# Where the gates' double steps fall among the units of dilated attention

## The chip, the core and the metric

One core of one Trainium2 chip runs the whole kernel. The metric is the device time of one execution in microseconds, the median of several runs. The core's engines are TensorE (PE for matmuls, PEld for its weight loads), VectorE (DVE), ScalarE (ACT), GpSimd (POOL) and SyncE (SP), which here only issues DMAs; ACT issues some too.

## What is computed

One hybrid decoder layer over 1024 positions of width 1024. One input projection feeds two attention groups of 8 heads each, latent attention (MLA) and a dilated sliding-window attention. Each group's output is multiplied by a SiLU gate, which is its own 512 columns of the projection. Both are concatenated, projected and added to the input under a LayerNorm.

```
h = x @ w_in
c_q, c_kv, k_rope, g_a, q_b, k_b, v_b, g_b = split(h)
y_a = mla_attention(c_q, c_kv, k_rope, ...) * silu(g_a)
y_b = dilated_attention(q_b, k_b, v_b) * silu(g_b)
mix = concatenate([y_a, y_b])
x   = layernorm(ALPHA * x + mix @ w_out)
```

## The kernel before

**Precision.** Float32 products are made from a high and a low part each, in three passes (high by high, high by low, low by high), so a product of one 128 x 512 tile over 1024 input rows takes 24 matmuls.

**Stages in time.** Projections of q, k, the latents and v fill the time up to about 224 us. Then comes the dilated stage, to about 410 us, in which the gates are made as well. MLA attention follows, and the output projection with the LayerNorm ends the kernel.

**The dilated stage.** The loop at the end of the dilated part goes over 32 units, `steps`, each a head pair `hp`, a half of the sequence `s` and a block `u` of 128 queries. For a unit, `dil_scores` makes 20 small matmuls into two PSUM banks (`Sd`, L607 and L611), and DVE adds the mask and takes the maximum (`td`, L615). `dil_expo` makes the exponentials on ACT (L621). One unit later `dil_inv`, `dil_high` and `dil_low` turn them into a high and a low part in float16 on ACT, POOL and DVE (tile `p`), and after each second unit SP issues one transposing DMA for both (`ptd<-p`, L659). Five units later, after each fourth, `dil_values` multiplies the transposed probabilities by the values (`Od`, L687), and DVE multiplies by the gate (L688). The PSUM pool holds the scores of two units.

**The gates.** A gate `gate(m, s)` is 24 matmuls of `gP` (L523) with the weights `wg` of column block m and the half s of x, then a tanh on ACT (L533) and a product on DVE (L534). It is a generator that yields after its first 12 matmuls and at its end, so a gate has two steps. `GATES` has 16 of them, in the order (4,0), (4,1), (5,0), (5,1), (6,0), (6,1), (7,0), (7,1), (0,0), (0,1), (1,0), (2,0), (3,0), (3,1), (2,1), (1,1): 32 steps, counted here from 0. From (1,0) on each gate needs other weights than the one before it, except (3,1). Weights of a block come in two loads of 256 KB, each issued on ACT's queue, rounded on ACT (`wg`, L76) and subtracted on POOL (L77). The first of the next block is asked for after the first step of a gate, the second at its end (`GLOAD`). Three tiles hold halves of weights, two hold raw loads; wg2 and wg1 are loaded a second time for (2,1) and (1,1).

**The fillers.** `fillers()` strings the gates together. When gate (3,0) has ended, the first halves of x are no longer needed, and at the next step `latents_load` has SP load the latents `c`, `u` and the tables into their place. After the last gate `latents_first` makes MLA's first keys and queries in four more steps. The loop over units calls `next(fill)` once or twice per unit:

```
            for _ in range(1 + (n % 3 == 0 and n < 24)):
                next(fill, None)
```

In the same loop SP is given the transposes `qq` and `kk` for the next head pair (four, in units 9 to 12 and 17 to 20) and the loads `vA` and `vB` (in units 12, 20 and 28, counted from 0; those of the first pair come ahead of the loop).

**What sets the order.** The program's order is a priority. A planner lays out each engine's instructions ahead of time by simulated readiness, so an instruction can pass others that it thinks not ready; on the chip each engine then runs its own list strictly in that order. DMAs are given completion semaphores in turn, and the issue of one can wait for an earlier one's landing.

Of the kernel before, what the change touches and what calls it, by code (L numbers as in the profile page):

```python
# [40 lines left out]
def tile_hybrid_layer(ctx, tc, xT, xres, w_c, w_c2, w_vr, w_k, w_q, w_g, w_u, w_o,  # L41
# [285 lines left out]
    def pow2_find(vmx, nm, bank_=bank):  # L327
        m1 = small.tile([P, 1], F32, name=nm + "m1", tag="vm")
        nc.vector.tensor_reduce(m1, vmx, AX.X, ALU.max)
        find_pow2(m1, 2.0 ** -40, nm, bank_)  # L330

    def pow2(j, nm, inv, bank_=bank):

        e = common_pow2(nm, bank_)
        r = small.tile([P, 1], F32, name=nm + "r", tag="vm4")
        nc.vector.reciprocal(r, e)
        nc.vector.tensor_scalar(scl[:, j, 0:1], r, 2.0 ** 14, None, ALU.mult)
        nc.vector.tensor_scalar(scl[:, j, 1:2], e, 2.0 ** -14 * inv, None, ALU.mult)
# [63 lines left out]
    def mla_scales():  # L402

        ee, d = fs[:, 4:5], fs[:, 5:6]
        nc.vector.tensor_mul(ee, es[:, 1:2], es[:, 3:4])
        nc.vector.tensor_scalar(scl[:, 0, 1:2], ee, 2.0 ** -5 / PSC, None, ALU.mult)
        nc.vector.tensor_scalar(fs[:, 6:7], scl[:, 4, 1:2], 2.0, None, ALU.mult)
        nc.vector.scalar_tensor_tensor(d, ee, 2.0 ** 10, fs[:, 6:7], ALU.mult, ALU.max)
        nc.vector.reciprocal(fs[:, 6:7], d)
        nc.vector.tensor_scalar(fs[:, 2:3], fs[:, 6:7], 2.0 ** 15, None, ALU.mult)  # L410
        nc.vector.tensor_scalar(fs[:, 3:4], fs[:, 2:3], ee, 2.0 ** -24, ALU.mult, ALU.mult)
        nc.vector.tensor_mul(fs[:, 6:7], es[:, 0:1], es[:, 2:3])
        nc.vector.tensor_scalar(fs[:, 7:8], fs[:, 6:7], d, -SC_MLA * 2.0 ** -19, ALU.mult, ALU.mult)

    def load_qk(hp):
        QQ[hp] = qqp.tile([P, 2, T], F16, name=f"qq{hp}", tag="qq")
        KK[hp] = b8.tile([P, 3, T], F16, name=f"kk{hp}", tag="kk")
        for s in range(2):
            sync.dma_start_transpose(QQ[hp][:, :, half(s)], q_d[half(s), hp * 2 * P:(hp + 1) * 2 * P])
            yield  # L420
            sync.dma_start_transpose(KK[hp][:, :, half(s)], k_d[half(s), hp * 3 * P:(hp + 1) * 3 * P])
            yield
# [132 lines left out]
    def load_v(hp):  # L555
        VA[hp] = four(f"vA{hp}", [P, NB, 2, P])
        sync.dma_start(VA[hp], v_d[1][:, :, hp].rearrange("n p l c -> p n l c"))
        VB[hp] = four(f"vB{hp}", [P, 2, 4, 2, P])
        for c in range(4):
            sync.dma_start(VB[hp][32 * c:32 * c + 32].rearrange("a j r l c -> a (j r) (l c)"),  # L560
                           v_d[1][2 * c:2 * c + 2].rearrange("j (r a) g l c -> a g (j r) (l c)", a=32)[:, hp])
# [30 lines left out]
    def dil_scores(u_):  # L592

        hp, s, u = u_
        i, ns = 4 * s + u, 3 + s
        stt = ST[u_] = small.tile([P, 2, 4], F32, name=f"st{hp}{i}", tag="st", bufs=4)
        TD[u_] = four(f"td{hp}{i}", [P, 2, 512], F32)
        S = [ps_s.tile([P, 512], F32, name=f"Sd{hp}{i}{e}", tag="S")[:, :ns * P] for e in range(2)]

        for cls in range(2):  # L600
            for w, e in JOBS:
                rows = ME[e] if w else slice(0, P)
                q, kk = QQ[hp][rows, e], KK[hp][rows, 2 if w else e]
                if not cls:
                    rhs = kk[:, (i - 1) * P:(i + 1) * P] if i else \
                        kk[:, 0:P].unsqueeze(1).broadcast_to([rows.stop - rows.start, 2, P])
                    nc.tensor.matmul(S[e][:, (ns - 2) * P:], q[:, i * P:i * P + P], rhs, start=(w == 0), stop=False)  # L607
                    continue
                for r in range(4):
                    rhs = kk.rearrange("p (i r a) -> p r i a", r=4, a=32)[:, r, 0:4 * s + 4]  # L610
                    nc.tensor.matmul(S[e][32 * r:32 * r + 32, :(ns - 2) * P],  # L611
                                     q[:, i * P + 32 * r:i * P + 32 * r + 32], rhs, start=False, stop=(w == 1))
        mk = mdil[:, u if i else 4, (4 - ns) * P:]
        for e in range(2):
            nc.vector.tensor_tensor_reduce(TD[u_][:, e, :ns * P], S[e], mk, dsc[:, 1:2], BIG,  # L615
                                           ALU.add, ALU.min, stt[:, e, 0:1])
# [7 lines left out]
    def dil_inv(u_):  # L624
        stt = ST[u_]
        nc.vector.tensor_scalar(stt[:, :, 2], stt[:, :, 1], 1.0 / PSC, None, ALU.mult)
        nc.vector.reciprocal(stt[:, :, 3], stt[:, :, 2])  # L627

    def dil_high(u_):
        hp, s, u = u_  # L630
        ns = 3 + s
        if u % 2 == 0:
            P16[hp, s] = hp_.tile([P, 2, 2, 2, ns * P], F16, name=f"p16{hp}{s}{u}", tag="p16")
        p16 = P16[hp, s][:, u % 2]
        for e in range(2):
            t, h, sc = TD[u_][:, e, :ns * P], p16[:, e, 0], ST[u_][:, e, 3:4]
            w = WHO[u][e]
            if w == "P":
                nc.gpsimd.tensor_scalar(t, t, sc, 1.0, ALU.mult, ALU.mult)  # L639
                sc = 1.0  # L640
            if w == "Q":
                nc.gpsimd.tensor_scalar(h, t, sc, 1.0, ALU.mult, ALU.mult)
            else:
                nc.scalar.activation(h, t, AF.Copy, scale=sc)  # L644

    def dil_low(u_):
        hp, s, u = u_
        ns, p16 = 3 + s, P16[hp, s][:, u % 2]
        if u == 0:
            PTD[hp, s] = tp.tile([P, 4, 4 * ns, P], F16, name=f"ptd{hp}{s}", tag=f"pT{s}")  # L650
        for e in range(2):
            t = TD[u_][:, e, :ns * P]
            if WHO[u][e] == "P":
                nc.gpsimd.tensor_sub(p16[:, e, 1], t, p16[:, e, 0])  # L654
            else:
                nc.vector.scalar_tensor_tensor(p16[:, e, 1], t, ST[u_][:, e, 3:4], p16[:, e, 0],
                                               ALU.mult, ALU.subtract)
        if u % 2:
            sync.dma_start_transpose(PTD[hp, s][:, u - 1:u + 1].rearrange("p u z c -> p (u z) c"),  # L659
                                     P16[hp, s].rearrange("p u e l w -> p (u e l w)"))  # L660
# [52 lines left out]
    def gen_kpe(s, part):  # L713

        if part == 0:
            KR[s] = four(f"krd{s}", [P, 4, 4, 32], F32)
            for z in range(4):
                gcopy(KR[s][:, :, z], kru.rearrange("p n t d -> p n (t d)")[:, s * 4:s * 4 + 4])
            return
        p = gbank(f"kpt{s}")  # L720
        for j in range(4):
            nc.tensor.transpose(p[:, j * P:(j + 1) * P], KR[s][:, j].rearrange("p z d -> p (z d)"), ident)
        k, sc = four(f"kpe{s}", [P, 2, 512]), fs[:, 2:3]
        nc.scalar.activation(k[:, 0], p, AF.Copy, scale=sc)
        nc.vector.scalar_tensor_tensor(k[:, 1], p, sc, k[:, 0], ALU.mult, ALU.subtract)
        sync.dma_start(kp_d[:, :, half(s)], k)
# [149 lines left out]
    for n in range(ND + 5):  # L876
        cur = steps[n] if n < ND else None
        old = steps[n - 1] if 1 <= n <= ND else None
        if n == 2:
            pow2_find(krm, "kr", gbank)  # L880
        if n == 5:
            pow2(4, "kr", 2.0 ** 14, gbank)
            mla_scales()
            nc.vector.tensor_scalar(scl[:, 0, 2:3], scl[:, 0, 1:2], 0.5, None, ALU.mult)
        if 8 <= n < 12:
            gen_kpe((n - 8) // 2, n % 2)
        if cur:
            if cur[1:] == (0, 1) and 0 < cur[0] < PAIRS - 1:
                qks = load_qk(cur[0] + 1)
            next(qks, None)  # L890
            if cur[1:] == (1, 0) and cur[0]:
                load_v(cur[0])
            dil_scores(cur)
        if old:
            dil_inv(old)
            dil_high(old)
            dil_low(old)
        if cur:
            for e in range(2):
                dil_expo(cur, e)  # L900
            for _ in range(1 + (n % 3 == 0 and n < 24)):
                next(fill, None)
        if n == ND + 3:
            for _ in fill:
                pass
        m = n - DV
        if 0 <= m < ND and m % 4 == 3:
            dil_values(*steps[m][:2])
# [165 lines left out]
    for i in ROWS:  # L1074
# [5 lines left out]
        for c in range(2):  # L1080
            if i in HALVED:
                n = 1 + (i == ROWS[-1])
# [121 lines left out]
```

## Time and profile before

| | |
|---|---|
| median of 3 runs | 649.92 us (649.61 to 652.25) |
| the profiled execution | 647.9 us |
| its span | 646.1 us, 11108 instructions |
| mean granted clock of TensorE | 0.977 |
| PE, DVE, ACT, POOL busy | 91%, 60%, 49%, 45% |
| dilated stage | about 224 to 410 us |

The shares are means over all stages; the stretch table and the timelines of the section on rows show the dilated stage by itself. A timeline's row is a group of like instructions that follow each other on an engine: start and length in us, engine, line, operation, names as out<-in, shape, count, and in brackets the idle time before it and what ended it. An engine with a q is its queue, which issues DMAs; the length of an issue includes the time in which it could not go on.

### The profile page before, as it was taken

How to read it: one execution, taken by the hardware profiler on the slowest of the kernel's cores; microseconds unless marked ns; L12 is line 12 of the kernel's file. 1: busy time of each engine (PE TensorE's matmuls, PEld its weight loads, DVE VectorE, ACT ScalarE, POOL GpSimd, SP SyncE). 2: the span in 40 equal slices, each digit the busy share in tenths (PEclk: the TensorE clock that was granted, in tenths of full speed). 3: DMA queues.
4: the chain of work that ended last, by engine and by line, in shares of the span. 5: the costliest groups of instructions: out<-in, count | busy, mean ns of one | idle time of the engine just before them, and what ended most of it. 6: DMA issues, size and time to landing. Idle time of an engine off the chain costs nothing.

```text
span 646.1 us, 11108 instructions
## 1 busy us (share of the span) xinstructions
PE 590.4 (91%) x4046; PEld 432.2 (67%) x4046; DVE 388.8 (60%) x888; ACT 318.2 (49%) x643; POOL 293.0 (45%) x324
## 2 busy tenths in 40 slices
PE   8999998999999899999996997877988868899995
PEld 5888886788999466776764544443545436678884
DVE  4415318480541686645645576589888995365696
ACT  4452136554221486555635565487978695240000
POOL 3284754265431227734643555283739556440000
PEclk9999999999999999999997998899989998999998
DMA  6666037796012779995999999559887899752042
GB/s 198 196 200 196 23 97 204 219 284 181 33 66 72 264 235 140 181 223 98 220 287 232 198 187 234 115 112 203 159 153 147 172 199 230 160 152 81 18 162 98
DMA packets 199527, 107.10 MB, mean 166 GB/s; under 512 B 157616, under 2 KB 176176, under 8 KB 199344
## 3 DMA queue, kind: packets, MB, share of 16 engines
q1 hardware_dynamic: 195872, 100.68, 66.4%
q10 hardware_dynamic: 3600, 5.71, 3.4%
q8 instruction: 31, 0.51, 0.3%
q14 instruction: 24, 0.20, 0.1%
HBM read 48.70 MB, written 18.87 MB: 105 GB/s over the span
## 4 chain that ended last, share of the span: by engine, by line
PE 60%; DMA 15%; DVE 12%; ACT 4%; issue 4%; POOL 3%; SPq 1%; DVEq 0%; POOLq 0%; ACTq 0%
PE gP L523 11%; PE op L958 7%; PE cP L254 7%; PE acc L169 7%; PE qkP L130 7%; DMA pT<-ph 5%; PE vbA L130 4%; PE vbB L130 4%; PE op L1087 3%; DVE ph L847 3%; DVE p L815 2%; PE Od L687 2%; PE qg L770 2%; DMA ptd<-p 2%; PE Sd L607 2%
## 5 line engine op out<-in xcount | busy, mean ns | idle before, releaser
L523 PE MATMUL gP<-x,wg 128*128 128x512 f32 x384 | 99.0, 406 | 5.7 <-ACT wg L76 5.2
L523 PEld LDWEIGHTS gP<-x,wg 128*128 128x128 f32 x384 | 70.7, 191 | 22.8 <-ACT wg L76 5.6
L958 PE MATMUL op<-wo,ys 128*128 128x512 f32 x288 | 70.3, 399 | 1.8 <-POOL wo L77 1.4
L958 PEld LDWEIGHTS op<-wo,ys 128*128 128x128 f32 x288 | 54.2, 191 | 15.5 <-POOL wo L77 2.4
L820 ACT ACTIVATE p<-p,sm 128x128 f32<-128x128 f32 (+3 forms) x64 | 49.1, 768 | 24.5 <-DVE sm L815 20.3
L809 PE MATMUL S<-k,q 128*128 128x512 f16 (+3 forms) x288 | 53.4, 328 | 7.4 <-DVE sm L815 7.4
L254 PE MATMUL cP<-x,wc 128*128 128x512 f32 x240 | 56.7, 395 | 0.0
L815 DVE CUSTOM_DVE_ANT_0 p<-S,mask,fs 128x128 f32<-128x128 f32 (+3 forms) x64 | 51.0, 807 | 7.8 <-POOL ph L845 5.7
L254 PEld LDWEIGHTS cP<-x,wc 128*128 128x128 f32 x240 | 44.7, 188 | 10.3
L621 ACT ACTIVATE td<-td,st 128x384 f32<-128x384 f32 (+1 forms) x64 | 42.2, 660 | 15.2 <-DVE st L615 15.0
L809 PEld LDWEIGHTS <-q 128*128 128x128 f16 x288 | 25.6, 98 | 33.3 <-issue 9.6
L639 POOL TENSOR_SCALAR td<-td,st 128x384 f32<-128x384 f32 (+1 forms) x32 | 21.9, 690 | 55.2 <-DVE st L627 43.1
L615 DVE CUSTOM_DVE_ANT_0 td<-Sd,mdil,dsc 128x384 f32<-128x384 f32 (+1 forms) x64 | 41.3, 678 | 9.0 <-PE Sd L611 8.7
L169 PE MATMUL acc<-wq,x 128*128 128x512 f32 x192 | 45.1, 395 | 0.8 <-DVE x L156 0.8
L845 POOL TENSOR_TENSOR ph<-p,ph 128x256 f16<-128x256 f32 (+3 forms) x32 | 37.2, 1173 | 18.1 <-ACT ph L838 16.5
L130 PE MATMUL qkP<-wk,x 128*128 128x512 f32 x192 | 44.5, 393 | 0.0
L859 PE MATMUL O<-pT,v 128*64 128x256 f16 (+1 forms) x480 | 31.0, 271 | 14.6 <-DMA pT<-ph 14.6
L169 PEld LDWEIGHTS acc<-wq,x 128*128 128x128 f32 x192 | 36.0, 188 | 10.5 <-DVE x L156 1.3
L130 PEld LDWEIGHTS qkP<-wk,x 128*128 128x128 f32 x192 | 36.0, 188 | 8.2
L847 DVE SCALAR_TENSOR_TENSOR ph<-p,sm,ph 128x128 f16<-128x128 f32 (+3 forms) x32 | 36.7, 1157 | 7.7 <-ACT ph L838 7.7
L859 PEld LDWEIGHTS <-v 128*64 128x64 f16 x480 | 26.8, 113 | 20.5 <-issue 15.0
L654 POOL TENSOR_TENSOR p<-td,p 128x384 f16<-128x384 f32 (+1 forms) x32 | 35.4, 1118 | 8.3 <-ACT p L644 8.0
(313 smaller groups left out, 1140.9 us busy)
## 6 DMA issues: line engine op xcount, KB each, us to landing
u<-in_w_u_dram SPq DMA_DIRECT2D x20, 256.0 KB, 3.2
v_d<-v SPq DMA_DIRECT2D x16, 256.0 KB, 2.1
wor<-in_w_o_dram SPq DMA_DIRECT2D x8, 512.0 KB, 4.2
xr<-in_xres_dram SPq DMA_DIRECT2D x16, 256.0 KB, 3.1
out_dram<-xr SPq DMA_DIRECT2D x16, 256.0 KB, 2.1
xr<-in_xT_dram SPq DMA_DIRECT2D x15, 256.0 KB, 3.2
k_d<-k SPq DMA_DIRECT2D x8, 384.0 KB, 4.4
c_d<-c SPq DMA_DIRECT2D x10, 256.0 KB, 2.4
```

Source lines behind the costliest of these rows:

```text
L130: nc.tensor.matmul(d, xs[k][i // 4][:, a, (i % 4) * P:(i % 4) * P + P], w8[k][:, b, o:o + w], **flags(k, KD, (a, b)))
L169: nc.tensor.matmul(acc[i], xs[k][i // 4][:, a, (i % 4) * P:(i % 4) * P + P], ws[:, b, :512], start=(k == 0 and (a, b) == (0, 0)), stop=(k ...
L254: nc.tensor.matmul(dst, ww(k, a, m), xs[k][s][:, b], **flags(k, KD, (a, b)))
L523: nc.tensor.matmul(p, wg[k // 4][:, a, (k % 4) * P:(k % 4) * P + P], xs[k][s][:, b], **flags(k, KD, (a, b)))
L615: nc.vector.tensor_tensor_reduce(TD[u_][:, e, :ns * P], S[e], mk, dsc[:, 1:2], BIG, ALU.add, ALU.min, stt[:, e, 0:1])
L621: nc.scalar.activation(t[:, :w], t[:, :w], AF.Exp, bias=ST[u_][:, e, 0:1], scale=-1.0, accum_out=ST[u_][:, e, 1:2])
L809: nc.tensor.matmul(S[:, lo:hi], q[:, a, qc], k[:, b, lo:hi], start=((a, b) == (0, 0)), stop=((a, b) == (1, 0)))
L815: nc.vector.tensor_tensor_reduce(t[:, :w], S[:, :w], M["mask"][:, T - w:], fs[:, 7:8], BIG, ALU.add, ALU.min, sm[:, 0:1])
L820: nc.scalar.activation(TT[u][:, :w], TT[u][:, :w], AF.Exp, bias=SM[u][:, 0:1], scale=-1.0, accum_out=SM[u][:, 1:2])
L847: nc.vector.scalar_tensor_tensor(p16[:, :, 1], t, SM[u][:, 3:4], p16[:, :, 0], ALU.mult, ALU.subtract)
L859: nc.tensor.matmul(O[ME[e], q0:], V[hp][:, kb, vh, ME[e]], rhs, **flags(kb, 2 * ch + 2, (vh, phl)))
L958: nc.tensor.matmul(op[i][:, half(c)], ys[k][a][:, i * P:(i + 1) * P], ws[k][b][:, half(c)], **flags(n_, KD, (a, b)))
```

## The change

The eight units in which the fillers make two steps are now the even ones of the first sixteen, and no longer every third one of the first twenty-four. Nothing else differs.

```diff
-            for _ in range(1 + (n % 3 == 0 and n < 24)):
+            for _ in range(1 + (n % 2 == 0 and n < 16)):
                 next(fill, None)
```

## Rows read from the trace of the kernel before

**Rows 1.** The page: busy us and shares by engine; the gate matmuls

```profile
PE 590.4 (91%) x4046; PEld 432.2 (67%) x4046; DVE 388.8 (60%) x888; ACT 318.2 (49%) x643; POOL 293.0 (45%) x324
L523 PE MATMUL gP<-x,wg 128*128 128x512 f32 x384 | 99.0, 406 | 5.7 <-ACT wg L76 5.2
```

**Rows 2.** Stretches: length, PE, PEld, DVE, ACT, POOL busy, clock, DMA share, GB/s

```profile
300.00:310.00 10.00, 10.00 (x75) 6.73 (x74) 5.63 (x19) 8.19 (x18) 6.62 (x7) 1.00 0.54 132
330.00:340.00 10.00, 10.00 (x117) 7.24 (x117) 4.32 (x12) 3.78 (x9) 2.91 (x4) 1.00 1.04 349
340.00:350.00 10.00, 5.15 (x74) 2.69 (x68) 4.10 (x12) 4.21 (x10) 2.92 (x3) 0.85 1.14 253
350.00:360.00 10.00, 9.28 (x101) 6.23 (x100) 5.58 (x20) 8.91 (x23) 7.92 (x9) 0.81 1.06 192
390.00:400.00 10.00, 6.92 (x81) 5.04 (x80) 5.38 (x14) 4.40 (x11) 5.85 (x7) 0.83 1.23 196
```

**Rows 3.** PE's timeline in the dilated stage

```profile
328.56 2.60 PE L523 MATMUL gP<-x,wg 128*128 128x512 f32 x10
...
334.28 0.61 PE L607 MATMUL Sd<-kk,qq 128*128 128x256 f16 x4
...
335.38 3.04 PE L523 MATMUL gP<-x,wg 128*128 128x512 f32 x12
338.35 1.53 PE L687 MATMUL Od<-ptd,vB 128*64 128x128 f16 x48
339.71 1.48 PE L687 MATMUL Od<-ptd,vA 128*64 128x128 f16 x30
...
348.25 1.22 PE L523 MATMUL gP<-x,wg 128*128 128x512 f32 x2 [4.85 <-ACT wg L76]
...
350.63 4.00 PE L523 MATMUL gP<-x,wg 128*128 128x512 f32 x10
...
361.68 2.52 PE L523 MATMUL gP<-x,wg 128*128 128x512 f32 x10
...
394.94 1.49 PE L687 MATMUL Od<-ptd,vB 128*64 128x128 f16 x24 [2.79 <-DMA ptd<-p]
```

**Rows 4.** SP's timeline: issues of DMAs around and after the c loads

```profile
323.46 1.72 SPq L421 DMA_TRANSPOSE kk<-k_d  x1
325.60 4.44 SPq L659 DMA_TRANSPOSE ptd<-p  x1
330.13 2.65 SPq L709 DMA_DIRECT2D c<-c_d  x5
...
356.01 20.25 SPq L659 DMA_TRANSPOSE ptd<-p  x3
```

**Rows 5.** ACT's timeline: issues and casts of gate weights

```profile
300.74 0.33 ACTq L117 DMA_DIRECT2D wg10r<-in_w_g_dram  x1
...
303.43 0.61 ACT L76 CAST wg<-wg10r 128x512 fp32r<-128x512 f32 x1
...
308.94 0.34 ACTq L117 DMA_DIRECT2D wg20r<-in_w_g_dram  x1
...
315.42 0.62 ACT L76 CAST wg<-wg20r 128x512 fp32r<-128x512 f32 x1 [2.43 <-DMA wg20r<-in_w_g_dram]
...
337.31 0.34 ACTq L117 DMA_DIRECT2D wg20r<-in_w_g_dram  x1
...
345.59 0.33 ACTq L117 DMA_DIRECT2D wg21r<-in_w_g_dram  x1
345.97 0.60 ACT L533 ACTIVATE g<-gP 128x512 f32<-128x512 f32 x1 [4.67 <-DMA vA<-v_d]
...
347.60 0.61 ACT L76 CAST wg<-wg20r 128x512 fp32r<-128x512 f32 x1
```

**Rows 6.** DMAs: landings of the probabilities' transposes; the loads of wg2

```profile
DMA to landing us min/median/max: 5.5/8.8/13.6
...
wg20r<-in_w_g_dram ACTq DMA_DIRECT2D x2, 256.0 KB, 6.3
```

## The prediction

> **What bounds the kernel now.** I read the page first: TensorE is busy for 91% of the span, and its dearest line is that of the gate matmuls, L523 [rows 1]. A mean over stages says little about a change to one of them, so next came the table of 10 us stretches over the dilated stage, which runs from 223.84 us to about 410 us [rows 2]. Two halves are to be seen there. Up to 340 us PE is full and its clock is whole, and between 300 and 310 us the DMA share is only 0.54. From 340 us on PE is busy for 5.15, 9.28 and, at 390 us, 6.92 us in stretches of ten, the granted clock there is 0.81 to 0.85, and the DMA share is 1.06 to 1.23. So the first half is bound by the sum of PE's work, whatever its order, and the second by what arrives. Last I read PE's, SP's and ACT's own timelines around 300 to 400 us [rows 3 to 5], for which wait ends last.
>
> PE's largest wait of the stage is 4.85 us before two gate matmuls at 348.25 us, for the cast of a gate weight; the next is 2.79 us at 394.94 us, for a transpose of probabilities [rows 3]. The first has a history. When gate (3,0) has ended (its last matmuls run from 328.56 to 331.16 us) its x tiles are free, and SP issues five c loads from 330.13 us, then tables, u, vA and vB [rows 3, 4]. The reload of wg2 is issued only at 337.31 us. The second part is issued at 345.59 us; ACT stands idle for 4.67 us around it, which end with vA's landing; and the cast of the first part, queued on ACT behind that issue and three activations, runs at 347.60 us [rows 5]. The stall is thus a weight load that stood behind other DMAs, once in the DMA engines and once in ACT's queue.
>
> **The change, part by part.** A step is half a gate: 12 matmuls, 335.38 to 338.35 us, 2.97 us. A unit's scores are 20 matmuls, 334.28 to 335.38 us, 1.10 us [rows 3]. There are 16 gates, so 32 steps, and both kernels make them in units 0 to 23, eight of them as second steps. I count steps done after unit n: before, n + 2 + floor(n/3); after, n + 2 + floor(n/2) up to n = 15 and n + 9 from there to n = 23. The difference is 1 at unit 2, 0 at unit 3, 1 at units 4 to 7, 2 or 1 from unit 8, 3 at unit 14, 2 at units 15 to 17, 1 at units 18 to 20, and 0 from unit 21. Nothing is added or removed: the 384 gate matmuls (99.0 us) stay [rows 1], as do 16 tanh, 16 products, 20 weight loads with their casts on ACT and subtractions on POOL. What moves is their place among the units, by at most three steps (8.9 us) of PE time.
>
> *Early stretch, 224 to 330 us.* PE does the same work and has almost no idle time to win: stretches read 10.00 of 10 [rows 2]. That bounds the gain here at about nothing. A loss needs PE to run dry at a double. Up to unit 8 both programs ask for almost the same. I put this at 0, with an upper bound under the rivals.
>
> *What follows the end of gate (3,0), call it T.* Its last step is number 25 (from 0). Before, it is made in unit 18 as the second of a double, and in the trace unit 19's scores also lie ahead of it; after, it is made in unit 17. So at T the after kernel has done the same gates but two units less, and T comes 2 x 1.10 = 2.2 us sooner, at about 329 us. What had been behind PE before T and now comes after it is those scores, 2.2 us, plus DMA: the transpose of units 16 and 17 (SP at 325.60 us, 4.44 us) and the last kk transpose (323.46 us, 1.72 us), 6.2 us of SP's queue [rows 4]. All of it meets the c burst. If PE sets the pace after T, the net is +2.2 - 2.2 = 0. If SP's queue and the DMA engines set it, it is +6.2 - 2.2 = +4.0 us. Rows for both: PE is busy for 9.28 of the ten us from 350, but SP's three transposes in a row take it from 356.01 to 376.26 us, and the DMA share is above 1.0 [rows 2, 4]. I take the middle, +2.0 us.
>
> On the price of a transpose the Trainium skill ("DMA: Bandwidth & Descriptors", section Latency and other measured facts) gives 261 GB/s for a DMA transpose; units 16 and 17 move 0.79 MB and a kk half 0.39 MB, so by that page an estimate is 3.0 + 1.5 = 4.5 us in place of 6.2, and the DMA-bound end would be +2.3 instead of +4.0. The trace disagrees for this kernel: the shortest landing of a ptd transpose was 5.5 us, the median 8.8 [rows 6], so the sum keeps SP's 6.2 us.
>
> *The stall on wg2.* Its full price: 4.85 us idle, and the slow clock behind it (0.81 to 0.85 granted over 340 to 360 us, a mix of the two levels, 2.4 and 1.2 GHz, after PE had stood still [rows 2]). The 10 gate matmuls at 350.63 us took 4.00 us against 2.52 at 361.68 us, 1.48 more; two gate matmuls 1.22 against 0.73 [rows 3]; with the scores between them about 2.4 us. So 7.25 us can be won and no more. After, the order is: step 26 and the first wg2 load in unit 18, step 27 and the second load in unit 19, then vA and vB (unit 20), then step 28, which needs wg2. Before, vA and vB stand ahead of the second load. So ACT's second blocked issue (4.67 us) should go or shrink. Against that, PE arrives sooner: between T and step 28 there are two steps and two or three units of scores, 8.1 to 9.2 us, where the present trace had from 331.16 us to the stall's start at 348.25 - 4.85 = 343.40 us, with Od's matmuls among it, 1.5 us on vB and 1.5 on vA [rows 3]; and the first load competes with the transposes counted above. Bounds: -7.25 us (it is there in time), and +3 us (Od's matmuls no longer cover it). I take -1.0, close to nothing, since the load's landing (median 6.3 us [rows 6]) is not itself made shorter.
>
> *Engines off the path.* The 20 casts (0.62 us) and subtractions keep their count; ACT's and POOL's idle time covers them before 340 us. SP is passed by nothing of the gates except through DMA: the weight loads go out on ACT's queue.
>
> Sum: 0 + 2.0 - 1.0 = +1.0 us. The profiled execution took 647.9 us, of which 646.1 are the span and 1.8 lie around it; so 648.9. The median of the runs shown, 649.92, is 2.0 above the profiled one; I carry that, and predict 650.9 us.
>
> **The rivals.** *Slower, the queue of the last third (chance 0.20).* SP and the DMA engines set the pace after T: +4.0 us and no gain at the stall, 653.9 us, up to 3 us more if Od no longer covers the stall, 656.9. It decides from the point at which SP has no free time between the c burst and the transposes of units 18 to 23. For: DMA shares above 1.0 from 330 to 360 us and at 390 us, and 2.79 us of PE's wait for a transpose. Against: PE has work of its own, 9.28 of ten us, once the stall is over [rows 2, 3].
>
> *Slower, weights late at the double of unit 14 (0.13).* Steps 21 and 22 follow each other there, and step 22 needs the first wg2, asked for after step 20. Between them PE has step 21 and one unit's scores, 4.1 us. With DMA quiet the load of wg1 was issued at 300.74 us and cast at 303.43, 2.7 us; with transposes beside it wg2's was issued at 308.94 and cast at 315.42, 6.5 us and 0.6 for the cast [rows 5]. So 3.0 us of wait, and with a clock fall of 2.4 us up to 5.4: 652.9 to 655.3 us. It decides from a landing above 3.5 us. Against: qq and kk transposes, which made that load slow, come only behind unit 15.
>
> *Faster, the stall goes (0.27).* The second wg2 load no longer blocks ACT behind vA, PE runs on at full clock and nothing else is late: -7.25 us at most, 642.7; half of it, 646.3. For: the blocked issue and the cast behind it [rows 5]. Against: a PE that runs ahead meets the transposes, which are as late as before.
>
> *The change does nothing (inside the forecast).* If the planner places a step only when its weights are there, the order comes out almost as it is, since the loads keep their distance of two steps: 649.9 us. For: PE had no idle time before 340 us although the loads vary from 2.7 to 6.5 us [rows 2, 5]. Against: from unit 8 on the two counts differ by two steps.
>
> **How the numbers follow.** Forecast and no effect together hold 0.40, and this is the likeliest case: 650.9 us, own range 647 to 653. The faster rival holds 0.27, the two slower ones 0.33. About 0.5%, 3.2 us, is what a measurement of this kernel can tell from no change, so these are also the chances of faster, same and slower. For 8 in 10 the range leaves out the far ends of the rivals: from 643.5 (nearly all of the stall won) to 657.5 (the late queue with a longer stall).
>
> **What would show it right or wrong.** In the trace of the changed kernel: PE full and at full clock until about 329 us, with steps two ahead of the present count at units 12 to 16 (if PE shows idle time before gate matmuls there, the second slower rival holds). The c loads about 1 to 2 us sooner, with a ptd transpose and a kk transpose behind rather than ahead of them. The wait before the first matmuls of gate (2,1): 4.85 us now; between 2 and 5 expected; near zero means the faster rival. ACT's second wg2 issue no longer ended by vA. Od's wait for a transpose, 2.79 us now, grown by several us means the slower rival. The last third measured from T to the first MLA scores tells the sum. The prediction is wrong if the planner moves work outside the dilated stage, which I count at zero since the program is the same from unit 24 on.

## The result and the profile after

The changed kernel took 655.16 us (median of 13 runs, 650.68 to 663.1), the kernel before in the same rounds 650.62 us (13 runs, 648.4 to 653.52). The ratio is 1.0063, with a 95% interval of 1.0035 to 1.0091: slower by 0.63%, some 4.1 us (2.3 to 5.9). It leaves out runs in a slower state, which some executions of any version show (one of these 13, at 663.1 us), and so lies below the quotient of the two medians. A second comparison gave 1.0059 [1.0025, 1.0092], with medians of 651.53 and 649.54 us. The forecast was +1.0 us; 655.16 us lies inside its range for 8 in 10, and above the 647 to 653 us that it called likeliest.

The profiled execution took 658.98 us, 3.8 us above its median, where that of before lies 2.7 us below its own. Part of this comes ahead of the stage: the first scores start at 226.70 us and not at 223.84 us, though both programs are the same up to there. In 14 profiles of this study that start lies between 223.84 and 227.50 us: at 226.57 or later in the seven with the change's doubles through unit 10, at 226.37 or sooner in the seven others. PE makes the same 1139 matmuls in the same order up to there in all of them. Whether the edit has a part in that difference was not tested, and what is said below of the loss leaves it out. So times of the stage are counted below from the first scores of the same execution, and a second profile of the changed kernel, called after2, stands beside the first.

The gate matmuls on the page of after (count, busy us, mean ns, idle time before them):

```profile
L523 PE MATMUL gP<-x,wg 128*128 128x512 f32 x384 | 101.1, 413 | 2.0 <-ACT wg L76 1.4
```

The waits of gate matmuls for a cast fell from 5.2 us to 1.4 us [rows 1], and yet the kernel got slower. The stretches of after that answer to [rows 2] (length, PE, PEld, DVE, ACT, POOL busy, clock, DMA share, GB/s):

```profile
340.00:350.00 10.00, 9.33 (x153) 6.38 (x151) 4.12 (x12) 3.43 (x10) 3.54 (x5) 1.00 1.02 392
350.00:360.00 10.00, 8.96 (x57) 4.26 (x58) 7.57 (x27) 8.40 (x21) 4.56 (x5) 0.60 1.16 264
```

From 340 to 350 us PE is now busy for 9.33 us of ten, where it was 5.15. From 350 to 360 us the granted clock is 0.60, where it was 0.81. PE's timeline shows what lies between (start, length, instruction, count, idle time ahead and what ended it):

```profile
309.66 0.73 PE L523 MATMUL gP<-x,wg 128*128 128x512 f32 x2 [0.64 <-ACT wg L76]
311.02 4.14 PE L523 MATMUL gP<-x,wg 128*128 128x512 f32 x10 [0.63 <-POOL wg L77]
...
333.76 3.04 PE L523 MATMUL gP<-x,wg 128*128 128x512 f32 x12
...
351.04 0.49 PE L607 MATMUL Sd<-kk,qq 128*128 128x256 f16 x2 [1.71 <-DVE st L615]
...
354.48 1.22 PE L523 MATMUL gP<-x,wg 128*128 128x512 f32 x2
...
357.97 4.99 PE L523 MATMUL gP<-x,wg 128*128 128x512 f32 x12
...
368.27 0.86 PE L687 MATMUL Od<-ptd,vB 128*64 128x128 f16 x24 [1.30 <-DMA ptd<-p]
...
398.73 0.30 PE L687 MATMUL Od<-ptd,vB 128*64 128x128 f16 x4 [2.44 <-DMA ptd<-p]
398.96 0.49 PE L607 MATMUL Sd<-kk,qq 128*128 128x256 f16 x2
...
408.48 1.45 PE L735 MATMUL kg<-c,u 128*128 128x512 f16 x6 [3.50 <-DVE qf L773]
```

Gate (3,0) ends at 336.80 us (the row at 333.76), 110.1 us after the first scores; before it was 107.3. The first matmuls of gate (2,1), at 354.48 us, wait for nothing: the stall of 4.85 us [rows 3] is gone. But a unit's scores have waited for DVE 3.4 us ahead of them, the clock is at its lower level of 1.2 GHz all the same, and 12 gate matmuls take 4.99 us. At the end of the stage four value matmuls (`Od`), with a wait of 2.44 us, stand ahead of the last unit's scores at 398.96 us. In [rows 3] such a wait, 2.79 us at 394.94 us, came behind them.

SP's and ACT's timelines of after, around the same times:

```profile
331.68 5.55 SPq L659 DMA_TRANSPOSE ptd<-p  x1
337.33 2.87 SPq L709 DMA_DIRECT2D c<-c_d  x4
...
343.32 11.08 SPq L659 DMA_TRANSPOSE ptd<-p  x1
```

```profile
344.64 0.33 ACTq L117 DMA_DIRECT2D wg20r<-in_w_g_dram  x1
345.07 0.94 ACT L644 ACTIVATE p<-td 128x384 f16<-128x384 f32 x2 [4.88 <-DMA c<-c_d]
```

In the kernel before, ACT's issues of the two loads of wg2 were both held: the second for 4.67 us, until vA had landed [rows 5], and the first for 4.25 us, until a load of c had landed, which the prediction's rows leave out. ACT's timeline of before:

```profile
337.75 0.61 ACT L644 ACTIVATE p<-td,st 128x384 f16<-128x384 f32 x1 [4.25 <-DMA c<-c_d]
```

The change took the second away: after's next issue, at 345.95 us, waits for nothing. The first stayed, at 4.88 us (5.27 in after2). PE had gate steps to make meanwhile in before. In after, the high parts of one unit and the exponentials of the next stand behind the held issue on ACT, DVE waits 4.57 us for these exponentials, and behind them in DVE's list stands the work that frees the banks for the scores at 351.04 us.

### The profile page after: what moved, and what is told of

It reads as the page before. It is cut to its first block, busy times and chain, and to the rows that moved or that the text cites. A ratio compares the mean times of both kernels' runs of the same rounds, so it can differ in the third digit from the quotient of the medians.

```text
span 656.0 us, 11105 instructions
## 1 busy us (share of the span) xinstructions
PE 602.4 (92%) x4046; PEld 438.8 (67%) x4046; DVE 390.7 (60%) x888; ACT 318.3 (49%) x643; POOL 295.4 (45%) x324
## 4 chain that ended last, share of the span: by engine, by line
PE 62%; DMA 15%; DVE 11%; issue 4%; ACT 4%; POOL 3%; SPq 1%; DVEq 0%; POOLq 0%; ACTq 0%
PE gP L523 10%; PE op L958 7%; PE acc L169 7%; PE cP L254 7%; PE qkP L130 7%; DMA pT<-ph 4%; PE vbA L130 4%; PE vbB L130 4%; DMA ptd<-p 3%; PE op L1087 3%; DVE ph L847 2%; DVE p L815 2%; PE Sd L611 2%; PE Od L687 2%; PE Sd L607 2%
## 5 line engine op out<-in xcount | busy, mean ns | idle before, releaser
L523 PE MATMUL gP<-x,wg 128*128 128x512 f32 x384 | 101.1, 413 | 2.0 <-ACT wg L76 1.4
L523 PEld LDWEIGHTS gP<-x,wg 128*128 128x128 f32 x384 | 72.3, 196 | 20.1 <-ACT wg L76 1.9
L169 PE MATMUL acc<-wq,x 128*128 128x512 f32 x192 | 47.2, 409 | 0.7 <-ACT wq L157 0.7
L859 PE MATMUL O<-pT,v 128*64 128x256 f16 (+1 forms) x480 | 32.8, 283 | 14.0 <-DMA pT<-ph 14.0
L169 PEld LDWEIGHTS acc<-wq,x 128*128 128x128 f32 x192 | 37.6, 197 | 10.7 <-ACT wq L157 1.6
L859 PEld LDWEIGHTS <-v 128*64 128x64 f16 x480 | 28.7, 118 | 19.9 <-issue 13.1
```

Of the source, the lines that this page charges most:

```text
L169: nc.tensor.matmul(acc[i], xs[k][i // 4][:, a, (i % 4) * P:(i % 4) * P + P], ws[:, b, :512], start=(k == 0 and (a, b) == (0, 0)), stop=(k ...
L523: nc.tensor.matmul(p, wg[k // 4][:, a, (k % 4) * P:(k % 4) * P + P], xs[k][s][:, b], **flags(k, KD, (a, b)))
L859: nc.tensor.matmul(O[ME[e], q0:], V[hp][:, kb, vh, ME[e]], rhs, **flags(kb, 2 * ch + 2, (vh, phl)))
```

## Experiments

All were timed in five rounds beside the kernel before. Four theories are named in the expectations. W: gate weights come late ahead of the end of gate (3,0). Q: SP's queue and the transposes behind it are late after that gate. O: the value matmuls of units 24 to 27, ahead of the last unit's scores, delay MLA's start. U: the packing of gate steps among the first units costs by itself.

**The change again, and each half of it.** after2 is the changed kernel. early has the change's count through unit 7 and returns to the old count from unit 9; mid has the old count through unit 9 and the change's from unit 11.

```diff
-            for _ in range(1 + (n % 2 == 0 and n < 16)):
+            for _ in range(1 + (n in (0, 2, 4, 6, 12, 15, 18, 21))):     # early
+            for _ in range(1 + (n in (0, 3, 6, 9, 10, 11, 12, 14))):     # mid
```

> The changed kernel once more, on the chip of this group, as the yardstick of the others. Both theories: about 1.006 times the kernel before. Theory W (weights late): from the first scores to the end of gate (3,0) PE shows waits for casts of gate weights and half-clock spells, together 2 to 4 us, where the kernel before has under 0.5. Theory Q (late queue): that stretch is within 1 us of before once the two units less are counted, and the loss lies between the end of (3,0) and the first MLA scores, in waits for transposes.

> The double steps of units 0 to 6 as in the changed kernel, the others as before (0, 2, 4, 6, 12, 15, 18, 21): the count of steps is that of before again from unit 12 on. Theory W: the weights of the later doubles (where each gate needs new ones) are asked for as before, so it equals the kernel before, 0 to +1 us. Theory Q: units 16 and later stand as before too, so it equals before as well. A loss of over 2 us here would mean the first eight units matter, which neither says.

> The kernel before up to unit 9, and the changed kernel's count of steps from unit 11 on (doubles at 0, 3, 6, 9, 10, 11, 12, 14). Theory W: the doubles stand still closer in units 9 to 14, so PE waits for gate weights there, the loss is that of the change or more, +4 to +7 us. Theory Q: the loss is that of the change, +4 us, and lies after gate (3,0).

Measured: after2 1.0059 [1.0025, 1.0092], early 1.0002 [0.9968, 1.0037], mid 1.0018 [0.9983, 1.0053]. Neither half shows a loss by itself; W and Q had both expected one of mid, whose interval still allows half a per cent. PE's timeline of after2 has the same two places as after:

```profile
347.93 0.49 PE L607 MATMUL Sd<-kk,qq 128*128 128x256 f16 x2 [2.08 <-DVE st L615]
...
364.44 0.86 PE L687 MATMUL Od<-ptd,vB 128*64 128x128 f16 x24 [0.49 <-DMA ptd<-p]
...
394.50 0.30 PE L687 MATMUL Od<-ptd,vB 128*64 128x128 f16 x4 [2.06 <-DMA ptd<-p]
```

Of the waits of 0.64 and 0.63 us at 309 to 311 us of after, after2 has one of 0.36 us and none of the lower clock behind it (the 4.14 us of ten gate matmuls). That spell belongs to one execution: after2 is slower without it.

**Weights asked for earlier (theory W).** In the changed kernel each block of gate weights is asked for one step sooner.

```diff
+        if (m, s) in GLOAD:
+            gate_load(GLOAD[m, s], 0)
...
-                    gate_load(GLOAD[m, s], 0)
+                    gate_load(GLOAD[m, s], 1)
...
-        if (m, s) in GLOAD:
-            gate_load(GLOAD[m, s], 1)
```

> The changed kernel with each gate weight asked for one step earlier in the program (the first half ahead of a gate, the second after its first step). Theory W: the waits for casts before the end of gate (3,0) go, and with them 2 to 4 us: 1.000 to 1.003 times the kernel before. Theory Q: no change against the changed kernel, about 1.006.

Measured: 1.0157 [1.0111, 1.0204], worse. W had expected 1.000 to 1.003. PE lost 4.15 us at 261.99 us, in a stretch that was full in after, and gate matmuls still waited 4.2 us for casts. So the edit brought waits of its own, and says nothing for or against W.

**No late weights at all, in both kernels.** a_nolate and b_nolate are the changed kernel and the one before, without the loads, casts and subtractions of wg1, wg2 and wg3. The six gates of these blocks are multiplied by wg0, so that part of the output is left out and the matmuls stay.

```diff
-    GLOAD = {g: h[0] for g, h in zip(GATES, GATES[1:]) if h[0] != g[0]}
+    GLOAD = {g: h[0] for g, h in zip(GATES, GATES[1:]) if h[0] != g[0] and h[0] not in (1, 2, 3)}
...
-        wg = WG[m]
+        wg = WG[0 if m in (1, 2, 3) else m]
```

> The changed kernel without the loads, casts and subtractions of the weights wg1, wg2, wg3 and their second loads: the gates of blocks 1, 2 and 3 are multiplied by wg0 (that part of the output is left out). Theory W: without these loads there is nothing to wait for, so it comes to within 1 us of the kernel before with the same left out. Theory O: it stays 2 to 4 us above that one. Theory Q (queue after gate (3,0)): the 10 loads of 256 KB less make both faster, the difference shrinks little.

> The kernel before without the same loads, casts and subtractions (gates 1, 2 and 3 multiplied by wg0; that part of the output is left out). The wait of 4.85 us for the second wg2 and the half-clock spell behind it go: by the prediction's price 4 to 7 us faster than the kernel before, 0.989 to 0.994. If the stall was covered by waits for transposes behind it, 0.997 to 1.000.

Measured: a_nolate 0.9953 [0.9919, 0.9988], b_nolate 0.9873 [0.9823, 0.9923]. First a stretch of b_nolate, then of a_nolate (columns as in [rows 2]):

```profile
340.00:350.00 10.00, 10.00 (x131) 7.77 (x134) 5.00 (x12) 5.20 (x11) 3.70 (x4) 1.00 1.20 255
```

```profile
340.00:350.00 10.00, 10.00 (x140) 7.26 (x139) 5.74 (x15) 3.82 (x9) 1.43 (x3) 1.00 1.15 285
```

PE is full at full clock in both, and from 350 to 360 us too, where the kernels with late weights have 5.15 and 9.33 of ten and clocks down to 0.60. This gives two results. The late weights, with their loads and casts, are worth 8.2 us to the kernel before (1.27% of 647.75; 5.0 to 11.5 by the interval). The prediction named 7.25 us as the most to win from one stall; the run takes ten loads, their casts and their subtractions away together and can't tell that stall from the rest. And the changed kernel is still slower by 0.8% (0.9953 over 0.9873; 645.76 against 641.14 us): theory W falls as the cause of the whole loss. Both make their last gate matmul 132.0 us after the first scores and start unit 28 at 142.2 us; they part behind that. In PE's timelines, first b_nolate, then a_nolate:

```profile
374.68 2.77 PE L687 MATMUL Od<-ptd,vB 128*64 128x128 f16 x48 [3.54 <-DMA ptd<-p]
```

```profile
380.13 2.77 PE L687 MATMUL Od<-ptd,vB 128*64 128x128 f16 x48 [4.80 <-DMA ptd<-p]
```

Less their first scores (225.51 and 227.50 us), these matmuls start at 149.2 and 152.6 us: the transposes they need land 3.5 us later in the changed kernel.

**The value matmuls and the last unit (theory O), from both sides.** a_sdfirst is the changed kernel with the value matmuls of units 24 to 27 queued behind unit 31's scores. b_odfirst is the kernel before with the same value matmuls ahead of most of unit 31's scores.

```diff
+            with tc.issue_after(LAST[0].ins) if m == 27 else ExitStack():   # a_sdfirst
+                dil_values(*steps[m][:2])
...
+            if n == 31:                                                     # b_odfirst
+                dil_values(*steps[27][:2])
```

> The changed kernel, with the value matmuls of the seventh group (units 24 to 27) queued on PE behind the scores of unit 31, as they stand in the kernel before; in the changed kernel four of them stand ahead of those scores and wait there for a transpose (2.4 and 2.1 us in its two traces). Theory O (that order delays unit 31, and with it the mask load and MLA's start): 2 to 3 us come back, 1.001 to 1.003 times the kernel before. Theory W (gate weights late before the end of gate (3,0)): nothing comes back, 1.005 to 1.007.

> The kernel before, with the same value matmuls put ahead of most of unit 31's scores. Theory O: 2 to 4 us slower, 1.003 to 1.006, since those scores now wait for the transpose. Theory W: no change, 0.999 to 1.002.

Measured: a_sdfirst 1.0109 [1.0063, 1.0156], b_odfirst 1.0128 [1.0083, 1.0173]. b_odfirst answers plainly. Its PE timeline:

```profile
398.48 1.49 PE L687 MATMUL Od<-ptd,vB 128*64 128x128 f16 x24 [4.56 <-DMA ptd<-p]
...
402.14 0.72 PE L607 MATMUL Sd<-kk,qq 128*128 128x256 f16 x2
```

Most of the last scores stand behind a wait for a transpose and the 48 value matmuls that it holds up, 4.56 and 3.7 us; they end 8.6 us later after the first scores than in the kernel before (176.9 against 168.3 us), and the kernel took 8.3 us more. Theory O had expected 2 to 4 us: so much more work stands ahead of the scores here than in the changed kernel, which has four value matmuls there. a_sdfirst shows what comes behind the last scores. Its DVE and SP timelines, and PE's:

```profile
397.24 0.91 DVE L923 MEMSET mask<- 128x1024 f32 x1 [0.28 <-DVE st L616]
...
408.65 0.69 DVE L774 SCALAR_TENSOR_TENSOR qf<-qg,mask 128x512 f32<-128x512 f32 x1 [5.60 <-DMA mask<-in_tabs_dram]
```

```profile
397.23 7.88 SPq L660 DMA_TRANSPOSE ptd<-p  x1
405.21 0.51 SPq L707 DMA_DIRECT2D mask<-in_tabs_dram  x1
```

```profile
409.39 2.72 PE L736 MATMUL kg<-c,u 128*128 128x512 f16 x6 [7.56 <-DVE qf L774]
```

DVE has masked the last scores by 397.24 us, 170.5 us after the first scores and 1.1 us sooner than after2 does. Only then is the mask's place free for MLA's table, which DVE needs for `qf`. Here SP took a transpose of 7.88 us first, and the table's load waited behind it until 405.21 us. Theory O had expected 1.001 to 1.003, and the run missed that by this wait of its own. Whether the value matmuls' place is worth anything to the changed kernel is therefore not settled by it. What it shows is a chain that the prediction did not have: last scores, mask, one load on SP, `qf`, MLA.

**The c burst one gate later (theory Q).** The call of `latents_load` follows gate (3,1), in both kernels.

```diff
-            if g == (3, 0):
+            if g == (3, 1):
```

> The changed kernel with the loads of the latents, u and the tables (the burst on SP's queue that follows gate (3,0)) given to SP one gate later, after gate (3,1). Theory Q (after gate (3,0), which now ends with two units fewer scored, the burst lies ahead of the transposes of pairs 8 and 9, which land some 20 us later than in the kernel before, and everything behind them on SP's queue stays late): the transposes of pair 8 land before the burst again, and the ratio falls from 1.006 to 1.002 or below. Theory U (the loss is the units' own, which stand behind more gate matmuls at the same time, whatever SP's queue holds): the ratio stays at 1.005 to 1.008. If the burst is only moved to where MLA needs it, its first keys wait longer and the ratio rises to 1.010.

> The kernel before with the same move of the burst by one gate. It is the other half of the pair: theory Q expects little here, 0.998 to 1.002, since pair 8 is ahead of the burst already; theory U expects 1.000. Were the move itself worth or costing something (the second load of wg2 no longer stands behind a load of c, the wait for it at about 343 us of 4.85 us gets shorter), it would show in this kernel as 0.993 to 0.997, and the changed kernel's ratio is then read against this one and not against 1.

Measured: a_latload 1.0034 [1.0, 1.0068], b_latload 0.9997 [0.9964, 1.0031]. The edit did not do what it was for. The planner put the burst where it had been, ahead of the transpose of units 16 and 17; SP's timeline of a_latload:

```profile
334.57 2.86 SPq L709 DMA_DIRECT2D c<-c_d  x4
...
340.62 10.87 SPq L659 DMA_TRANSPOSE ptd<-p  x1
```

That is 107.9 us after the first scores, against 107.7 in after2. So Q wasn't tried, and a_latload stands as a near copy of the changed kernel, with 0.34% where after and after2 had 0.63 and 0.59%; the three intervals overlap. Its profile tells one thing more, in PE's timeline:

```profile
348.23 0.49 PE L607 MATMUL Sd<-kk,qq 128*128 128x256 f16 x2 [1.72 <-DVE st L615]
...
353.05 3.00 PE L523 MATMUL gP<-x,wg 128*128 128x512 f32 x12
...
364.26 0.89 PE L687 MATMUL Od<-ptd,vB 128*64 128x128 f16 x24 [4.18 <-DMA ptd<-p]
```

The wait for DVE is that of after, 1.72 us, but the clock did not fall, and the 12 gate matmuls took 3.00 us in place of 4.99. The value matmuls then waited 4.18 us for their transposes, where after2 waited 0.49, and started 137.6 us after the first scores, where after2 did at 137.9. What PE kept by its clock in this profile it gave back at the transposes, which landed 137.5 and 137.8 us after the first scores.

**Two more places for the double steps.** front10 has the change's doubles through unit 10 and the last two in units 17 and 20, so that gate (3,0) ends in unit 18 as before. six is the kernel before without the doubles of units 18 and 21.

```diff
+            for _ in range(1 + (n in (0, 2, 4, 6, 8, 10, 17, 20))):     # front10
+            for _ in range(1 + (n % 3 == 0 and n < 18)):                # six
```

> Double steps in units 0, 2, 4, 6, 8, 10, 17 and 20: the changed kernel's count of gate steps through unit 11, then one step a unit until 17, so that gate (3,0) ends in unit 18, with as many units scored as in the kernel before. If the loss needs gate (3,0) to end two units sooner (theory Q, and any cause that lies behind it): 0.998 to 1.002. If the packing of gate steps among the first eleven units costs it by itself (theory U): 1.004 to 1.008.

> The kernel before without its last two double steps (units 18 and 21): gate (3,0) ends in unit 19, one unit later than before, the four steps after it come one to a unit, and the last gate and MLA's first keys come two units later. It goes the other way from the change. Theory Q and theory U both expect it not slower: with single steps about gate (2,1) its weights have a unit more to come, the wait of 4.85 us and part of the 6.8 us of half clock behind it go, 0.992 to 0.998. A rival: the last gates and MLA's first keys then fall among the last units, whose scores and transposes come later by as much: 1.002 to 1.006.

Measured: front10 1.0083 [1.0044, 1.0121], six 0.9996 [0.9962, 1.003]. front10 is slower with gate (3,0) in its old unit, so the loss does not need that gate two units sooner. But it has waits of its own; first PE's timeline of front10, then of six:

```profile
336.56 0.73 PE L523 MATMUL gP<-x,wg 128*128 128x512 f32 x2 [2.78 <-ACT wg L76]
```

```profile
352.77 1.38 PE L687 MATMUL Od<-ptd,vB 128*64 128x128 f16 x22 [8.42 <-DMA ptd<-p]
```

The wait of 2.78 us in front10 stands just behind its double of unit 17, where after has none, so front10 doesn't prove theory U. six lost the wait of 4.85 us at gate (2,1), as expected, and took one of 8.42 us for transposes at about the same point of the stage (128.6 us after the first scores); its time stayed, where 0.992 to 0.998 had been expected.

## Why the prediction came out as it did

**What the end follows.** Two events near the end of the stage were tried as marks: the end of the last unit's scores, and the start of the value matmuls of units 24 to 27, which wait for a transpose. Worked out from the traces, in us after the first scores of each execution ("behind" counts the last unit's scores, of 20, that PE makes after that start):

```
kernel      unit 28   unit 31's    values 24-27   their   behind   end of    from that start
            starts    scores end   start          wait             span      to the end
before      150.4     168.3        171.1          2.79     0       422.3     251.2
early       149.3     166.6        169.6          2.99     0       421.4     251.7
six         152.3     165.2        167.1          1.90     0       420.2     253.0
b_latload   148.7     166.6        169.8          3.22     0       419.4     249.6
front10     154.8     169.4        173.7          4.27     0       424.8     251.1
a_ask       157.6     172.0        178.0          4.41     0       429.5     251.4
mid         148.2     168.1        166.1          2.07    20       420.3     254.3
after       153.8     174.4        172.0          2.44    20       429.3     257.3
after2      150.1     169.9        167.9          2.06    20       422.7     254.7
a_latload   151.3     171.0        169.0          1.93    20       424.4     255.3
b_odfirst   150.5     176.9        172.1          4.56    14       429.3     257.2
b_nolate    142.2     160.4        161.8          none     0       412.2     250.4
a_nolate    142.2     163.4        164.2          0.73     0       418.1     254.0
a_sdfirst   151.0     168.7        168.8          0.10     0       427.4     258.6
```

From the end of unit 31's scores it is 251.8 to 255.3 us to the end of the span in 12 of 14 profiles; the two others are a_ask (257.5) and a_sdfirst (258.7), where the table's load came late on SP. The time up to that point varies by 16.5 us, so the mark shows a large loss; its spread of 3.5 us is nearly the loss of the change. The five kernels within 0.2% of before end these scores at 165.2 to 168.3 us, mean 167.0; the three profiles of the changed order at 169.9 to 174.4, mean 171.8: 4.8 us later.

The other mark says why. In the first six rows PE has made the last scores before it waits for the transpose, and from the start of the value matmuls to the end it is 249.6 to 253.0 us. In the five rows from mid to b_odfirst all or most of these scores stand behind the first value matmuls, and it is 254.3 to 257.3 us. The start itself comes no later in the changed order, at 169.7 us on the mean of three against 169.4 of before, early, six and b_latload. What the three lose to these four, 4.4 us, lies behind this start, where the order differs. mid has the same order and is not slower, since its value matmuls start at 166.1 us, the earliest of the rows with late weights. front10 lost by another way: it has the old order, and its transpose came at 173.7 us.

The profile's own chain of work that ended last (start, length, what) shows the two orders, first in before, then in after:

```profile
384.45 10.45 DMA ptd<-p
394.94 3.53 PE Od L687 x48
...
401.58 2.96 DMA mask<-in_tabs_dram
...
405.38 2.72 PE kg L735 x6
```

```profile
388.21 10.47 DMA ptd<-p
...
398.73 0.30 PE Od L687 x4
...
400.21 0.89 PE Sd L611 x14
401.09 2.88 PE Od L687 x44
...
409.66 2.96 DMA mask<-in_tabs_dram
...
413.46 2.72 PE kg L735 x6
```

The mask in both is the second load of MLA's table, which SP issues behind a transpose. In early, six and b_latload the chain runs as in before; in after2, mid and a_latload it goes from the transpose through the four value matmuls and the last scores to the table's first load. In before the last scores are not on it. They were made while the transpose was under way, and end at 392.16 us; in PE's timeline:

```profile
391.63 0.53 PE L611 MATMUL Sd<-kk,qq 128*32 128x256 f16 x12
```

DVE then needs the value matmuls for a product that stands ahead of `qf` in its list. DVE's timeline of before, and of after:

```profile
398.50 0.75 DVE L688 SCALAR_TENSOR_TENSOR g<-Od,scl,g 128x512 f32<-128x512 f32 x1 [3.67 <-PE Od L687]
...
399.38 0.67 DVE L773 SCALAR_TENSOR_TENSOR qf<-qg,mask 128x512 f32<-128x512 f32 x1
```

```profile
407.74 0.69 DVE L773 SCALAR_TENSOR_TENSOR qf<-qg,mask 128x512 f32<-128x512 f32 x1 [2.78 <-DMA mask<-in_tabs_dram]
```

In before the first load of the table, asked for when the last scores were done, had landed by 398.6 us, while DVE stood for the value matmuls: the two waits ran side by side. In after they stand one behind the other: PE's wait for the transpose comes ahead of the last scores, and DVE then waits 2.78 us for the table. In b_odfirst the same order was set by hand in the kernel before, in a stronger form, and the kernel got slower. The opposite test, the changed kernel with the scores ahead, was to be a_sdfirst. There the last scores were done at 168.7 us and the value matmuls waited 0.10 us, as hoped, but SP's queue then held the table. So the order accounts for the loss in these profiles, and no run that undoes it has shown it.

**Where the time goes.** PE's own count says it in another way: time since the first scores, less the usual time of the matmuls that PE had started by then (from one's start to the next one's, for each kind its median in the kernel before). What is left is waiting, lower clock and the cost of switching between small groups.

```
us since the first scores       90     110    130    190    240    end
before                          6.1    8.2   15.7   28.9   37.8   66.9
early, mid, six, b_latload
  (lowest to highest)        5.7-7.5 7.1-9.8 14.0-16.3 27.6-28.2 36.3-37.0 64.0-66.0
after                          10.7   12.1   17.1   35.4   44.8   73.9
after2                          7.4    9.0   15.6   29.4   39.6   67.3
a_latload                       7.7    9.5   13.3   30.1   40.4   69.0
```

Against the mean of the five, the three changed profiles are 2.4 us behind at 90 us (1.4 with after2 and a_latload alone), level at 130 us (-0.1), 3.5 behind at 190 and 4.7 at the end. The middle stretch won, the last third lost more. The first profile of after, 3.8 us above its median, weighs in this: with after2 and a_latload alone it is 1.0 us ahead at 130 us, 1.6 behind at 190 and 2.7 at the end.

Now the prediction's steps, one by one.

- *Early stretch, put at 0.* Near, but too low: 1.4 us by after2 and a_latload. The gate matmuls up to the end of gate (3,0) were to stay as they are; grouped by line, first before, then after2, up to that point (count, busy us, mean ns, idle before):

```profile
L523 PE MATMUL gP<-x,wg 128*128 128x512 f32 x312 | 77.9, 399 | 0.0
```

```profile
L523 PE MATMUL gP<-x,wg 128*128 128x512 f32 x312 | 78.4, 400 | 0.4 <-POOL wg L77 0.4
```

  The same matmuls were busy for 0.5 us more, and there are 0.4 us of wait; the value matmuls by then cost another 0.5 us, in 11 pieces between other work where before had 8. PE full is no proof that order is free.

- *T 2.2 us sooner.* Wrong. T came 110.1 (after), 106.7 (after2) and 107.3 us (a_latload) after the first scores, 107.3 before, with 18 units scored by then in place of 19 and a half (the prediction counted all 20 score matmuls of unit 19 ahead of T, and 11 were). So one and a half units of scores were pushed behind T and little was gained for it; the c burst came 1.4 us (after2) to 4.3 us (after) later after the first scores, and not 1 to 2 us sooner.

- *What follows T, +2.0 between 0 and +4.0.* The order came as forecast, the transpose of units 16 and 17 behind the burst: its issue takes SP from 343.32 to 354.40 us in after, where [rows 4] had it at 325.60 us, ahead of the burst. The value matmuls of the group behind it start 137.6 to 141.6 us after the first scores in the three changed profiles, and at 133.2 us before (357.07 us). The place was right. It is not shown that these 4.4 us and more reach the end: the run meant to undo them left SP's order as it was, and the transpose of units 26 and 27, which the chain goes through, came no later than in the old order.

- *The stall on wg2, -1.0 between -7.25 and +3.* The stall went wholly, and so did ACT's second held issue, as forecast. But the first one stayed, and the prediction gave it no wait: PE, which in before had gate steps to make meanwhile, now waited 1.71 us (after) and 2.08 us (after2) for DVE behind it, and the granted clock over 350 to 360 us was 0.60 and 0.53. Over the stretch from 90 to 130 us the three changed profiles gained 2.5 us on the mean of the five, where this term and the one before it together said +1.0.

- *"The same from unit 24 on", counted at zero.* This is the step that failed. The gate steps are indeed the same there, but the planner set four value matmuls, with their wait of about 2 us, ahead of the last unit's scores, which the kernel before makes while it waits. From the start of these value matmuls to the end the changed order took 4.4 us longer. By PE's count the three profiles lost 3.6 us between 130 and 190 us after the first scores (2.6 with after2 and a_latload alone), the stretch in which this lies.

The range held the measured time, but not for the reasons it was built on: the early stretch cost 1.4 us in place of nothing, T came hardly sooner, the stall was won in part, and what made the kernel slower lay in a stretch that the sum counted at nothing. So the number was in part luck: it is the width of the range, drawn for the rivals, that took it in.

Of the rivals, "the queue of the last third" had the size, +4.0 us and more, but not the sign named for it: PE's waits for transposes did not grow (3.5 us in all before, 3.7 in after and 3.8 in after2, from 250 us to the end of the stage); they came to stand ahead of the last scores. "Weights late at the double of unit 14" did not show: PE waited a step or two ahead of it, at gate (1,0), 1.27 us with 1.6 us of lower clock behind it in after and 0.4 us in after2, and not at the double; a_nolate rules late weights out as the whole cause. The faster rival had its premise, the stall's end, and not its gain.

What stays open: whether the changed kernel with the old order of these value matmuls would be as fast as before, since a_sdfirst met another wait; why a_nolate, with the old order, is slower than b_nolate all the same (its value matmuls of units 20 to 23 waited for a transpose that landed 3.5 us later); and whether the later start of the stage is part of the loss. No version that computes the whole layer ran faster than before by more than a measurement can tell; early, six, mid and b_latload are its equals.

## What to carry to other kernels

Before a wait on the busiest engine is priced, follow the chain of work that ended last to the event that the rest hangs on, here a late transpose, and ask of each edit whether that event moves and what the engine still has to do once it has come. Work that was made during a wait and now stands behind it can be lost time, though no wait got longer. A wait that ends ahead of another one that is due anyway is not worth its length: one of 4.85 us was removed in two ways (the change, six), and neither was faster. And count as moved not just the steps whose index differs, but all that a planner places by readiness behind them.

## What the runs showed of the chip that was not expected

- After nearly equal short waits of PE the granted clock did not do the same: behind 1.71 and 2.08 us (after, after2) 12 gate matmuls were at the lower level in whole or in part, behind 1.72 us (a_latload) the clock stayed whole and 12 of them took 3.00 us. One profile can't price a short wait's clock.
- ACT stood idle at the issue of a weight load until a DMA of another queue had landed, with activations queued behind: 4.25 us (a load of c) and 4.67 us (vA) in before, 4.88 us (c) in after, 5.27 us (c) in after2. What PE had to do meanwhile made the difference: beside the first of these it was full (10.00 of ten from 330 to 340 us [rows 2]), behind the last two it waited 1.71 and 2.08 us.
- The first scores of the stage come between 223.84 and 227.50 us in 14 profiles, with PE's matmuls ahead of them the same and in the same order. Differences of 3 us between two single profiles mean nothing here unless they are counted from a common event.
